# Attention work queued by products, values last, and a Strassen pair in both output projections of a two-layer decoder trunk

## The chip, the cores and the metric

The kernel runs on one core of one Trainium2 chip. The time is device microseconds of one execution; three runs of the kernel before are given by their median. TensorE (PE) multiplies, ScalarE (ACT) and VectorE (DVE) work on tiles in SBUF and PSUM, SyncE (SP) and GpSimd (POOL) issue the transfers here.

## The reference, cut to what matters

256 tokens of width 2048 pass through two layers, all in float32. What the kernel computes is, in order:

```python
hn = rms_norm(h, norm_mix[0])                       # layer 0
proj = hn @ w_in                                    # 2048 x 6144: RG-LRU and HGRN2 heads
mixed = concatenate([lru, hgrn], -1)                # each 1024 wide
h = h + mixed @ w_out                               # output projection, 2048 x 2048
h = h + square(relu(rms_norm(h) @ w1)) @ w2         # 2048 x 8192, 8192 x 2048
hn = rms_norm(h, norm_mix[1])                       # layer 1
q, k, v = split(hn @ w_qkv)                         # 16 heads of 128; partial rotary on q, k
s = q @ k.T * 128 ** -0.5 + log(multiplicity)       # three dilated windows merged into one mask
h = h + (softmax(s) @ v) @ w_o                      # output projection, 2048 x 2048
h = h + square(relu(rms_norm(h) @ w1b)) @ w2b
out = rms_norm(h, final_norm)
```

## The kernel before, in words

**Split operands.** TensorE multiplies in a rounded float32 form, so each operand is split into a high part and the rest. Weights come in units of 128 x 2048 float32 (1 MB): SP loads them into `raw` (three buffers), ScalarE casts the high part (`hi`, L103), VectorE subtracts it (`lo`, L104). Each block of 128 x 128 activations by 128 x 512 weights takes three matmuls (high by high, high by low, low by high), all issued by `mm` (L182). `fetch` prepares units two to three ahead, in the order of the list `units`.

**Two ways to multiply.** `tokens` takes one group of 512 output columns: four units, and for each unit and each half of the tokens (`j`) four blocks, twelve matmuls of 512 columns. These twelve are called a **product** here. Two groups cost 2 x 4 x 2 = 16 products. `blocks` takes a pair of column groups, `n0` and `n0 + 1`, and multiplies the first half of the inner dimension (blocks 0 to 7) by a seven-product scheme of Strassen's kind, the second half (units 8 to 15, called "n" in the lists) plainly: 7 + 8 = 15 products. The seven are called a, t1, t2, c, t3, d and t4. Their weights are sums of units: VectorE adds some (L131), an accumulating DMA of POOL's queue adds others (L143, L149). Their activations are sums too, the "forms" (`formx` for the first MLP matrix and the attention, `formh` for the second): four combinations of 128 x 128 blocks on VectorE (`combos`, L574 to L577) and a split (`part_forms`, L570 and L571). `ORDERS` lists the products: a, t1, then one n, t2, c, the other n, t3, d, n, t4, n. When a product of the seven is complete, an *event* reads its PSUM bank. In `first` (w1) `hold` copies it away on ScalarE (L697) into tiles `y1`, `y2`, `y4`; in `second` (w2) `to_x` adds it to the residual `xres` on VectorE (L732).

**The stages.** The recurrent layer runs to about 337 us. `out_project` then runs four groups of `tokens` against w_out. After each group the residual is added (L588), and `to_features` is put in the list `later`: it transposes the residual on TensorE (`turn`, L185) into a bank `pl` (two banks), scales by the gain and splits into `bufa` (L225 and L226), and for the first two groups also makes the forms by way of a tile `z` of the name `y21` (one buffer, L609). The MLP runs four quarters, each of two pairs by w1 and two by w2. Between them `to_h` transposes the squared activations into `bufb` and makes `formh`. At the end of layer 0 each finished group is turned into features for the attention (`done`).

**What sets the order.** `later` holds Python functions that issue instructions. `flush` runs all that were there when a plain unit began, after that unit: whole `to_features` calls, two halves at once, go between two products. Matmuls through `mm` and transposes through `turn` keep the order in which they are issued; each engine's other instructions are placed by a scheduler with priorities (`urgent` puts them early, `stream` puts the weights' work somewhat early).

**The attention.** Six pairs by w_qkv in the order `ATTENTION = "qvqqvq"`: a "q" pair gives queries and keys of four heads, a "v" pair the values of eight. `queries_keys` applies the rotary on VectorE (L876 to L880) and transposes on TensorE (L883), with a copy to `qT` and `kT` (L884). `scores` takes two matmuls (L891 and L892), adds the mask (L894), takes the maximum (L898), the exponential on ScalarE, and the division on VectorE (L902); it transposes the probabilities into the bank `pd` (L905) and copies them to `pT` (L907). `mix` multiplies by the values into the bank `po` (L913 and L914) and splits into `bufb` (L915). These transposes and matmuls are called on the engine directly, so the scheduler places them, without `urgent`. The residual waits in DRAM (`kept`) and POOL brings it back (L933). Then come `out_project` with w_o, the second MLP and the final norm.

Of the kernel before, what the change touches and what calls it, by code (L numbers as in the profile page):

```python
# [36 lines left out]
TC_ID, TC_LNC, TC_FREQ = 0, 128, 512  # L37
NTAB = 528
# [3 lines left out]
def trunk_kernel(ctx, tc, x, xtok, cols, tab, masks, pos, fin, w_in, w_gate, w_out, w_qkv, w_o, w1, w2, out):  # L42
# [28 lines left out]
    def plan2(src, i):  # L71
        for what, u in ORDERS[src is not w1]:
            units.append((src, None if u is None else i + u, what, i))
# [51 lines left out]
    def combine(u, src, i, what, i0):  # L125
# [115 lines left out]
    nc.sync.dma_start(tab_, tab)  # L241
    msk = cst.tile([P, NLEV, P], I8, name="msk")
    nc.sync.dma_start(msk, masks)
    ident = tab_[:, TC_ID:TC_ID + P]
    lnc = tab_[:, TC_LNC:TC_LNC + 384]
# [68 lines left out]
    def tokens(src, i0, mov, kgs=(0, 1, 2, 3), by_k=False):  # L314
        ks = range(KB)
        ps = [pmm.tile([P, 512], F32, name="p") for _ in range(2)]
        for g in kgs:
            w = unit(src, i0 + g)
            order = [(j, i) for i in range(4) for j in range(2)] if by_k else \
                [(j, i) for j in range(2) for i in range(4)]  # L320
            for j, i in order:
                k = ks[4 * g + i]
                h, l = w.part(i * 512, 512)
                xh = mov[:, k, j * P:j * P + P]
                xl = mov[:, k, S + j * P:S + j * P + P]
                first, last = g == kgs[0] and i == 0, g == kgs[-1] and i == 3
# [6 lines left out]
    def tokens_group(src, i0, rt=None, by_k=False, kgs=(0, 1, 2, 3)):  # L333
        ps = tokens(src, i0, bufa, kgs, by_k)
# [14 lines left out]
    wk = mixers.enter_context(tc.tile_pool(name="wk", bufs=2))  # L349
    nrm = FirstNorm()  # L350
# [3 lines left out]
    rs = tmp.tile([P, S], F32, name="nr", bufs=1)  # L354
# [238 lines left out]
    def to_features(n, gname, forms=None):  # L593
        def work():
            with urgent():
                for half in range(2):
# [6 lines left out]
                    if forms is None:  # L603
                        for i in range(2):
                            split_to(bufa[:, k + i], p[:, i], col(gname, k + i))
                        continue
                    z = pair.tile([P, 2, 2, P], F32, name="y21")
# [8 lines left out]
        later.append(work)  # L616

    def out_project(src, gname, kgs):
# [6 lines left out]
    nrm = out_project(w_out, "nmlp0", (2, 3, 0, 1))  # L625
    cosT = cst.tile([P, 2, 16], F32, name="cosT")
    sinT = cst.tile([P, 2, 16], F32, name="sinT")

    def blocks(src, i0, n0, mov, forms, events, final):
        plain = lambda j, k: (mov[:, k, j * P:j * P + P], mov[:, k, S + j * P:S + j * P + P])  # L630
# [20 lines left out]
        for what, u in ORDERS[src is not w1]:  # L651
# [8 lines left out]
            due = len(later)  # L660
# [4 lines left out]
            flush(due)  # L665

    def to_h(n, tiles):
# [20 lines left out]
        later.append(work)  # L688

    def first(i0, n0):  # L690
# [23 lines left out]
        def final(n, j, bank):  # L714
            with urgent():
                if (n, j) == (1, 1):
                    keep["delta"] = bank
                elif (n, j) == (0, 1):
                    y = pair.tile([P, 512], F32, name="y21")
# [6 lines left out]
        blocks(w1, i0, n0, bufa, formx, {"a": hold("y1", 2), "t1": hold("y4"), "t2": hold("y2"), "t3": u3}, final)  # L726

    def second(i0, n0, nrm, r2, r2n, done, gains):
        def to_x(bank, j, n, r, last):
            at = slice(n * 512, n * 512 + 512)  # L730
            with urgent():
                V.scalar_tensor_tensor(xres[:, j, at], bank, r[:, j:j + 1], xres[:, j, at], op0=OP.mult, op1=OP.add)  # L732
# [8 lines left out]
        def u3(bank):  # L741
# [3 lines left out]
        blocks(w2, i0, n0, bufb, formh,  # L745
               {"a": lambda b: to_x(b, 0, n0, r2, False), "t1": lambda b: to_x(b, 1, n0 + 1, r2, False),
                "t2": u2, "t3": u3},
               lambda n, j, b: to_x(b, j, n0 + n, r2, (n, j) != (1, 1)))
        done(n0)

    def mlp(layer, nrm, nxt, gname):
        fing = []

        def gains():
            for n, name in enumerate(("y1", "y1", "y2", "y4")):
                fing.append(pair.tile([P, 512], F32, name=name, bufs=2 if n < 2 else 1))
# [8 lines left out]
        for q in range(4):  # L765
# [17 lines left out]
            for n in (0, 2):  # L783
                second(layer * 64 + q * 16, n, ends, r2, r2n, done, gains if ends and not gname and not n else None)
        return fing

    def rotary():
# [19 lines left out]
        V.tensor_scalar(sinT, cosT, math.pi, -2.0 * math.pi, op0=OP.is_gt, op1=OP.mult)  # L807
        V.tensor_tensor(cosT, cosT, sinT, OP.add)
        V.tensor_scalar(cosT, cosT, PI, -PI, op0=OP.min, op1=OP.max)
        V.tensor_scalar(sinT, ang, PI, -PI, op0=OP.min, op1=OP.max)  # L810
        lut(cosT, cosT, AF.Sin)
        lut(sinT, sinT, AF.Sin)
# [8 lines left out]
    wk = mixers.enter_context(tc.tile_pool(name="wk2", bufs=2, reuse_waits="tile"))  # L821
    rt = rstd(nx1)
# [3 lines left out]
    def token_pair(i, c0, ready, raw=()):  # L826
        out_ = lambda n, j: xres[:, j, c0 + 512 * n:c0 + 512 * n + 512]
# [39 lines left out]
    def queries_keys(i, raw=()):  # L867
        turned = [wk.tile([P, 4, S], F32, name="qT", bufs=2), wk.tile([P, 4, S], F32, name="kT", bufs=2)]

        def ready(n, j, o):  # L870
# [3 lines left out]
            with urgent():  # L874
                b = wk.tile([P, 4, 2, 16], F32, name="rb", bufs=2)
                V.tensor_tensor(b[:, :, 0], r[:, :, 1], per(sinT), OP.mult)  # L876
                V.tensor_tensor(b[:, :, 1], r[:, :, 0], per(sinT), OP.mult)
                for two in range(2):
                    V.tensor_tensor(r[:, :, two], r[:, :, two], per(cosT), OP.mult)
                    V.tensor_tensor(r[:, :, two], r[:, :, two], b[:, :, two], OP.add if two else OP.subtract)  # L880
# [3 lines left out]
                A.copy(turned[n][:, :, j * P:j * P + P], p)  # L884
# [4 lines left out]
    def scores(q, k):  # L889
        ps_ = psc.tile([P, 384], F32, name="pl", bufs=2)  # L890
        T.matmul(ps_[:, :P], q[:, :P], k[:, :P], start=True, stop=True)  # L891
        T.matmul(ps_[:, P:], q[:, P:], k, start=True, stop=True)  # L892
        s = wk.tile([P, 384], F32, name="as", bufs=2)
        V.scalar_tensor_tensor(s, ps_, P ** -0.5, lnc, op0=OP.mult, op1=OP.add)  # L894
        nm = wk.tile([P, 2], F32, name="nm", bufs=2)
        ll = wk.tile([P, 2], F32, name="ll", bufs=2)
        for j, sl in enumerate((slice(0, P), slice(P, 384))):
            V.tensor_reduce(nm[:, j:j + 1], s[:, sl], AX.X, OP.max, negate=True)  # L898
            lut(s[:, sl], s[:, sl], AF.Exp, bias=nm[:, j:j + 1], accum_out=ll[:, j:j + 1])
        V.reciprocal(ll, ll)  # L900
        for j, sl in enumerate((slice(0, P), slice(P, 384))):
            V.tensor_scalar(s[:, sl], s[:, sl], ll[:, j:j + 1], None, op0=OP.mult)  # L902
        pt = psc.tile([P, 384], F32, name="pd", bufs=1)
        for j in range(3):
            T.transpose(pt[:, j * P:j * P + P], s[:, j * P:j * P + P], ident)  # L905
        st = wk.tile([P, 384], F32, name="pT", bufs=5)
        A.copy(st, pt)  # L907
        return st

    def mix(hd, st):  # L910
        vs = slice(D // 2 + (hd % 8) * P, D // 2 + (hd % 8) * P + P)
        po = psc.tile([P, S], F32, name="po", bufs=1)
        T.matmul(po, xres[:, 0, vs], st[:, :S], start=True, stop=False, skip_group_check=True)  # L913
        T.matmul(po[:, P:], xres[:, 1, vs], st[:, S:], start=False, stop=True, skip_group_check=True)  # L914
        split_to(bufb[:, hd], po)  # L915

    waiting, hd = [], 0
    for i, what in enumerate(ATTENTION):
        if what == "v":
            token_pair(i, D // 2, lambda *_: None)  # L920
        else:
            q, k = queries_keys(i, ((0, 0), (1, 1)) if not i else ())
            for h in range(4):
                waiting.append((hd, scores(q[:, h], k[:, h])))
                hd += 1
                if i and ATTENTION[:i].count("v") * 8 >= hd:
                    mix(*waiting.pop(0))
        if what == "v":
            while waiting:
                mix(*waiting.pop(0))  # L930
    for n in range(4):
# [5 lines left out]
    nrm = out_project(w_o, "nmlp1", (0, 1, 2, 3))  # L937
# [48 lines left out]
LINE = 64  # L986
# [4 lines left out]
ORDERS = (_A + (("n", 6),) + _B + (("n", 7),) + _C, _A + (("n", 7),) + _B + (("n", 6),) + _C)  # L991
T4_DMA = lambda w1, w2, w_qkv: (w1, w_qkv)
# [3 lines left out]
def _tables():  # L996
# [9 lines left out]
    tab = np.zeros((P, NTAB), np.float32)  # L1006
# [17 lines left out]
def _layout(a):  # L1024
# [32 lines left out]
    for what in ATTENTION:  # L1057
# [14 lines left out]
        "w_in": c(np.concatenate(w_in)), "w_gate": c(w_gate), "w_out": c(toks(n(a["rec_w_out"][0]))),  # L1072
        "w_qkv": c(np.concatenate(w_qkv)), "w_o": c(toks(n(a["attn_w_o"][0]))),
# [20 lines left out]
```

## Time and profile before

| what | value |
|---|---|
| runs of the kernel | 2190.3, 2188.92, 2190.04 us (median 2190.04) |
| profiled execution | 2187.37 us, span 2185.4 us |
| granted clock of TensorE, mean | 0.997 |
| TensorE / weight loads / VectorE / ScalarE / GpSimd busy | 2142.0 / 1814.9 / 1808.3 / 1301.5 / 60.1 us |
| HBM read / written | 475.44 / 4.19 MB |

The profile records one execution. A row of a timeline has start, duration, engine, line, operation, output and inputs with shapes; a bracket holds the idle time before it and what ended that. In the view of waits a row reads: who waited, for whom, total us, times, longest. Line numbers are those of the kernel before. "p", "pt", "po", "pd" and "pl" are PSUM banks. Matmuls overlap: one of 512 columns lasts 0.39 us in the records, while the next begins 0.23 us after its start.

### The profile page before, as it was taken

To read this page: it belongs to the slowest core of one execution; us is meant where nothing else is said; L and a number is where in the kernel's file an instruction comes from. 1 tells how busy PE (TensorE), PEld (TensorE's weight loads), DVE (VectorE), ACT (ScalarE), POOL (GpSimd) and SP (SyncE) were. 2 spreads that over 40 slices of the span, in tenths; PEclk is the share of its full clock that TensorE was granted. 3 is DMA by queue.
4 is the path that set the end of the run, shared out by engine and by line. 5 is a ranking of instruction groups with operands and counts; after the bars stand their busy time and mean duration, and the time that the engine had idled before them with its cause. 6 is when DMAs were issued, how large, how long until landed. Compare 5 with 4: busy or idle time off the path is not lost.

```text
span 2185.4 us, 27134 instructions
## 1 busy us (share of the span) xinstructions
PE 2142.0 (98%) x10778; PEld 1814.9 (83%) x10778; DVE 1808.3 (83%) x1972; ACT 1301.5 (60%) x1408; POOL 60.1 (3%) x77
## 2 busy tenths in 40 slices
PE   9999999999999999999989999999999999999997
PEld 8999998878888888888778888778888888888886
DVE  8766787779879889889888787767897898898897
ACT  7444485566566466566566565555655755755664
POOL 0000000000000000000000000000000000000000
PEclk9999999999999999999999999999999999999999
DMA  8444445577777777677766767747767777777873
GB/s 316 157 161 165 149 158 207 183 242 236 232 234 247 225 240 241 234 241 234 241 221 212 241 211 213 250 157 222 230 219 256 239 222 245 251 226 225 262 236 130
DMA packets 68734, 481.39 MB, mean 220 GB/s; under 512 B 7680, under 2 KB 8448, under 8 KB 11648
## 3 DMA queue, kind: packets, MB, share of 16 engines
q1 hardware_dynamic: 58176, 410.90, 51.6%
q0 software_dynamic: 10144, 68.16, 16.1%
q8 instruction: 84, 1.38, 0.3%
q10 hardware_dynamic: 288, 0.61, 0.1%
q14 instruction: 42, 0.34, 0.0%
HBM read 475.44 MB, written 4.19 MB: 219 GB/s over the span
## 4 chain that ended last, share of the span: by engine, by line
PE 86%; ACT 6%; DVE 4%; issue 2%; DMA 1%; SPq 0%; DVEq 0%; ACTq 0%
PE p L182 57%; PE po L182 11%; PE pd L182 10%; PE pt L182 4%; ACT hi L103 4%; DVE lo L104 2%; PE pl L185 2%; PE pl L453 1%; DMA raw<-in_w 0%; ACT y L701 0%; DMA raw<-in_w_qkv 0%; ACT formh L570 0%; ACT y L697 0%; ACT y L702 0%; PE pl L892 0%
## 5 line engine op out<-in xcount | busy, mean ns | idle before, releaser
L103 ACT CAST hi<-raw 128x2048 fp32r<-128x2048 f32 (+2 forms) x432 | 673.4, 1577 | 550.7 <-PE p L182 347.3
L104 DVE TENSOR_TENSOR lo<-raw,hi 128x2048 fp32r<-128x2048 f32 (+2 forms) x432 | 804.9, 1874 | 197.2 <-ACT hi L103 195.4
L182 PE MATMUL p<-hi,bufb 128*128 128x512 f32 x1408 | 450.1, 391 | 4.8 <-DVE xall L732 2.6
L182 PE MATMUL p<-hi,bufa 128*128 128x512 f32 x1360 | 439.6, 391 | 12.2 <-ACT y L697 7.9
L182 PEld LDWEIGHTS p<-hi,bufb 128*128 128x128 f32 x1408 | 264.2, 188 | 63.6 <-DVE xall L732 6.1
L182 PEld LDWEIGHTS p<-hi,bufa 128*128 128x128 f32 x1360 | 254.9, 188 | 69.7 <-ACT y L697 11.3
L104 DVE TENSOR_TENSOR lo<-s,hi 128x2048 fp32r<-128x2048 f32 x114 | 260.8, 2288 | 28.2 <-ACT hi L103 25.9
L182 PE MATMUL p<-lo,bufb 128*128 128x512 f32 x704 | 274.4, 390 | 1.2 <-DVE lo L104 1.2
L182 PE MATMUL p<-lo,bufa 128*128 128x512 f32 x680 | 266.5, 392 | 3.8 <-DVE lo L104 3.7
L103 ACT CAST hi<-s 128x2048 fp32r<-128x2048 f32 x114 | 218.1, 1913 | 57.4 <-PE po L182 24.0
L182 PE MATMUL p<-bufa,hi 128*128 128x256 f32 x1280 | 240.9, 287 | 0.1
L182 PEld LDWEIGHTS p<-bufa,hi 128*128 128x128 f32 x1280 | 200.7, 191 | 0.4 <-DVE hz L400 0.3
L182 PE MATMUL p<-bufa,lo 128*128 128x256 f32 x640 | 182.7, 285 | 0.0
L182 PEld LDWEIGHTS p<-lo,bufb 128*128 128x128 f32 x704 | 132.2, 188 | 28.5 <-DVE lo L104 1.6
L182 PEld LDWEIGHTS p<-lo,bufa 128*128 128x128 f32 x680 | 127.7, 188 | 32.7 <-DVE lo L104 6.9
L131 DVE TENSOR_TENSOR s<-s,raw 128x2048 f32<-128x2048 f32 x54 | 123.4, 2286 | 12.3 <-DMA raw<-in_w_qkv 9.8
L182 PEld LDWEIGHTS p<-bufa,lo 128*128 128x128 f32 x640 | 122.4, 191 | 0.0
L182 PE MATMUL p<-hi,formx 128*128 128x512 f32 x352 | 115.9, 390 | 0.0
L104 DVE TENSOR_TENSOR lo<-t,hi 128x2048 fp32r<-128x2048 f32 x38 | 87.0, 2289 | 17.7 <-ACT hi L103 17.7
L131 DVE TENSOR_TENSOR s<-raw,t 128x2048 f32<-128x2048 f32 x38 | 86.9, 2286 | 0.0
L182 PE MATMUL pd<-hi,bufa 128*128 128x512 f32 x256 | 84.8, 392 | 0.0
L182 PE MATMUL po<-hi,bufa 128*128 128x512 f32 x256 | 84.8, 392 | 0.0
(290 smaller groups left out, 3075.6 us busy)
## 6 DMA issues: line engine op xcount, KB each, us to landing
raw<-in_w SPq DMA_DIRECT2D x224, 1024.0 KB, 4.9
raw<-in_w_in SPq DMA_DIRECT2D x46, 1024.0 KB, 4.8
raw<-in_w_qkv SPq DMA_DIRECT2D x42, 1024.0 KB, 6.6
t<-in_w SPq DMA_DIRECT2D x32, 1024.0 KB, 5.4
t<-in_w POOLq DMA_DIRECT2D x32, 1024.0 KB, 8.6
raw<-in_w_out SPq DMA_DIRECT2D x16, 1024.0 KB, 4.7
s<-in_w POOLq DMA_DIRECT2D x16, 1024.0 KB, 8.7
raw<-in_w_o SPq DMA_DIRECT2D x16, 1024.0 KB, 4.8
```

The source lines that it names most:

```text
L103: A.copy(h, w)
L104: V.tensor_tensor(l, w, h.bitcast(F32), OP.subtract)
L131: V.tensor_tensor(held[to], held[x], held[y], OP.add)
L182: chain[:] = [after(T.matmul(*args, **kw), chain)]
L185: chain[:] = [after(T.transpose(out_, in_, ident), chain)]
L453: T.matmul(pl[:, j], kq[:, js], halves(qp[:, js], c, True), start=True, stop=True)
```

## The change

The change has these parts.

- `later` becomes a queue with due times. `clock` counts products, `put_off(wait, f)` makes `f` due `wait` products later, and `flush` after each product runs what is due, at most one function in `blocks` and two in `tokens`. `to_features` is put off by 2 products and each of its halves is a function of its own, `to_h` by 5.
- `out_project` runs two groups by `tokens` and the last two as one pair by `second` (with w_out or w_o, in the Strassen scheme). The forms of `bufb` are made in `formh` during the first group. The "t4" weights come by the accumulating DMA for all but w2.
- `y4` and `y21` get two buffers each; room is made by taking the mask table and some tiles out of the constant pool. All sources use one order of products.
- The attention's order is "qqvqqv". Transposes of queries and keys are put off by 5 products, the scores of head h of a pair by 6 + 2h, the transposes of the probabilities by 3 more, the mixes by 2 after the values, all through `mm` and `turn`. The softmax is marked urgent; its division moves to ScalarE. A mix's result is copied by ScalarE before the split, and mixes alternate between two banks. Rotary takes four operations for six. Every second query/key pair keeps one block in a spare tile.

The diff, cut to its core:

```diff
-    units.extend((w_out, 4 * n + g) for n in range(4) for g in (2, 3, 0, 1))
     for layer in range(2):
...
-            plan(w_o, 16)
+        plan((w_out, w_o)[layer], 8)
+        plan2((w_out, w_o)[layer], 8)
...
-        if ahead == ("t4",) and src not in T4_DMA(w1, w2, w_qkv):
+        if ahead == ("t4",) and src is w2:
             add("s", "s", "d")
...
-        if what == "c" and src in T4_DMA(w1, w2, w_qkv):
+        if what == "c" and src is not w2:
             nc.gpsimd.dma_start(held["s"], src[i0 + 1], accum_op=OP.add)
...
-    def flush(due=None):
-        todo = later[:due]
-        del later[:due]
-        for f in todo:
-            f()
+    clock = [0]
+
+    def put_off(wait, *fs):
+        later.extend((clock[0] + wait, f) for f in fs)
+
+    def flush(products, most):
+        clock[0] += products
+        later.sort(key=lambda x: x[0])
+        while most and later and later[0][0] <= clock[0]:
+            later.pop(0)[1]()
+            most -= 1
...
-            flush()
+                if i == 3 and (j or not by_k):
+                    flush(2 if by_k else 1, 2)
...
-                    z = pair.tile([P, 2, 2, P], F32, name="y21")
+                    z = pair.tile([P, 2, 2, P], F32, name="y21", bufs=2)
...
-        later.append(work)
+        put_off(WAIT_X, *(lambda half=half: work(half) for half in range(2)))
...
-        for n in range(4):
-            add_res(tokens(src, 4 * n, bufb, kgs), n, nrm)
-            to_features(n, gname, formx if n < 2 else None)
+        def forms(k):
+            z = pair.tile([P, 2, 2, P], F32, name="y21", bufs=2)
+            h, l = (bufb[:, k + off:k + off + 2, c * S:c * S + S].bitcast(F32) for c in range(2))
+            V.tensor_tensor(z.rearrange("p i j c -> p i (j c)"), h, l, OP.add)
+            a11, a21, a12, a22 = (z[:, i, j] for i in range(2) for j in range(2))
+            combos(a22, a11, a21, a12, a11, a21, a12, a22)
+            part_forms(formh, k // 2, 1, slice(0, 4), z.rearrange("p i j (one c) -> p one (i j) c", one=1))
+
+        put_off(4, *(lambda k=k: forms(k) for k in range(0, 8, 2)))
+        for n in range(2):
+            add_res(tokens(src, 4 * n, bufb, ks=[(k + off) % KB for k in PAIRED]), n, nrm)
+            to_features(n, gname, formx)
+        second(src, 0, 2, nrm, None, OP.subtract, lambda n: to_features(n, gname), None, off)
         return nrm
...
-            flush(due)
+                flush(1, 1)
...
-        later.append(work)
+        put_off(WAIT_H, work)
...
-        blocks(w1, i0, n0, bufa, formx, {"a": hold("y1", 2), "t1": hold("y4"), "t2": hold("y2"), "t3": u3}, final)
+        blocks(w1, i0, n0, bufa, formx, {"a": hold("y1", 2), "t1": hold("y4", 2), "t2": hold("y2"), "t3": u3}, final)
...
-                for h in range(4):
-                    T.transpose(p[:, h], t[:, h], ident)
-                A.copy(turned[n][:, :, j * P:j * P + P], p)
+                for h in range(4):
+                    turn(p[:, h], t[:, h])
+                with urgent():
+                    A.copy(turned[n][:, :, j * P:j * P + P], p)
+
+            put_off(WAIT_Q, turns)
...
-        for j, sl in enumerate((slice(0, P), slice(P, 384))):
-            V.tensor_scalar(s[:, sl], s[:, sl], ll[:, j:j + 1], None, op0=OP.mult)
...
+                for j, sl in enumerate((slice(0, P), slice(P, 384))):
+                    A.activation(s[:, sl], s[:, sl], AF.Copy, scale=ll[:, j:j + 1])
+            put_off(wait, lambda: turned(s))
...
-        po = psc.tile([P, S], F32, name="po", bufs=1)
-        T.matmul(po, xres[:, 0, vs], st[:, :S], start=True, stop=False, skip_group_check=True)
-        T.matmul(po[:, P:], xres[:, 1, vs], st[:, S:], start=False, stop=True, skip_group_check=True)
-        split_to(bufb[:, hd], po)
+        po = psc.tile([P, S], F32, name="pd" if hd % 2 else "po", bufs=1)
+        mm(po, xres[:, 0, vs], st[:, :S], start=True, stop=False, skip_group_check=True)
+        mm(po[:, P:], xres[:, 1, vs], st[:, S:], start=False, stop=True, skip_group_check=True)
+        z = tmp.tile([P, S], F32, name="z")
+        with urgent():
+            A.copy(z, po)
+        split_to(bufb[:, hd], z)
...
             token_pair(i, D // 2, lambda *_: None)
+            put_off(2, *(lambda h=h: mix(h, ready_.pop(h)) for h in range(hd - 8, hd)))
...
-                waiting.append((hd, scores(q[:, h], k[:, h])))
+                put_off(WAIT_Q + 1 + 2 * h, head(hd, q[:, h], k[:, h], WAIT_S))
...
+    restore(0)
+    restore(1)
+    put_off(2, lambda: restore(2), lambda: restore(3))
...
-ATTENTION = "qvqqvq"
+ATTENTION = "qqvqqv"
...
+WAIT_H, WAIT_X, WAIT_Q, WAIT_S = 5, 2, 5, 3
...
-ORDERS = (_A + (("n", 6),) + _B + (("n", 7),) + _C, _A + (("n", 7),) + _B + (("n", 6),) + _C)
+ORDERS = _A + (("n", 7),) + _B + (("n", 6),) + _C
```

More of the change, by code (lines that the diff above doesn't have):

```diff
@@ L325, in tokens @@
                 xl = mov[:, k, S + j * P:S + j * P + P]
-                first, last = g == kgs[0] and i == 0, g == kgs[-1] and i == 3
+                first, last = g == 0 and i == 0, g == 3 and i == 3
                 mm(ps[j], xh, h, start=first, stop=False)
@@ L593, in to_features, with work @@
     def to_features(n, gname, forms=None):
-        def work():
+        def work(half):
             with urgent():
-                for half in range(2):
+                if True:
                     p = psc.tile([P, 2, S], F32, name="pl", bufs=2)
@@ L718, in final @@
                 elif (n, j) == (0, 1):
-                    y = pair.tile([P, 512], F32, name="y21")
+                    y = pair.tile([P, 512], F32, name="y21", bufs=2)
                     relu2(0, 1, y, bank)
@@ L783, in mlp @@
             for n in (0, 2):
-                second(layer * 64 + q * 16, n, ends, r2, r2n, done, gains if ends and not gname and not n else None)
+                second(w2, layer * 64 + q * 16, n, ends, r2, r2n, done, gains if ends and not gname and not n else None)
         return fing
@@ L826, in token_pair, with out_ @@
     def token_pair(i, c0, ready, raw=()):
-        out_ = lambda n, j: xres[:, j, c0 + 512 * n:c0 + 512 * n + 512]
+        spare_ = wk.tile([P, 512], F32, name="q0", bufs=1) if not c0 and ATTENTION[:i].count("q") % 2 else None
+        def out_(n, j):
+            return xres[:, j, c0 + 512 * n:c0 + 512 * n + 512] if spare_ is None or (n, j) != (0, 0) else spare_
         def put(n, j, r=rt):
@@ L875, in ready @@
                 b = wk.tile([P, 4, 2, 16], F32, name="rb", bufs=2)
[L876 to L880, printed above, removed]
+                c = wk.tile([P, 4, 2, 16], F32, name="rc", bufs=2)
```

133 lines of the change are left out of this document (71 added, 62 removed).

## The prediction

> **What bounds the kernel now.** I read the page first: which engine is full, and which one the chain that ended last runs through.
>
> ```profile
> span 2185.4 us, 27134 instructions
> ...
> PE 2142.0 (98%) x10778; PEld 1814.9 (83%) x10778; DVE 1808.3 (83%) x1972; ACT 1301.5 (60%) x1408; POOL 60.1 (3%) x77
> ...
> PE 86%; ACT 6%; DVE 4%; issue 2%; DMA 1%; SPq 0%; DVEq 0%; ACTq 0%
> ```
>
> The reader is to see TensorE busy nearly throughout and on 86% of the chain. Two things can shorten this kernel: fewer matmuls, or fewer of TensorE's own waits. VectorE at 83% is second and matters below. The chain in order of time gives the price of matmuls:
>
> ```profile
> 559.25 5.44 PE p L182 x24
> ...
> 1106.52 4.38 PE po L182 x12
> ```
>
> Twenty-four 128x512 matmuls take 5.44 us, so one **product** of twelve takes 2.72 us. The second row is a product that took 4.38; I return to it. Next the view of TensorE's waits (total, times, longest), then the same view from 1145 to 1430 us, the attention, and last from 1065 to 1145, the passage into it:
>
> ```profile
> PE p L182 <- ACT y L697: 7.9, 8, 1.0
> PE pl L185 <- DVE bufa L226: 5.6, 1, 5.6
> ...
> PE p L182 <- DVE bufa L226: 3.6, 3, 1.4
> ```
>
> ```profile
> PE pl L891 <- ACT qT L884: 2.0, 1, 2.0
> PE p L182 <- ACT bufb L222: 1.9, 3, 1.4
> PE p L182 <- DVE lo L104: 1.4, 2, 1.1
> PE po L913 <- ACT pT L907: 0.9, 1, 0.9
> PE po L913 <- DVE bufb L223: 0.8, 1, 0.8
> ```
>
> ```profile
> PE p L182 <- DVE xall L732: 1.3, 1, 1.3
> PE p L182 <- DVE lo L104: 1.2, 1, 1.2
> ```
>
> The waits are few and named; nearly each has an edit of the change against it.
>
> **The change part by part.** The sum is made against the profiled execution: 2187.37 us, its span of 2185.4 and 2.0 around it. The median of the runs, 2190.04, lies 2.7 higher; I add that at the end.
>
> *Products (A).* A pair of column groups costs 16 products by `tokens` (2 groups x 4 weights x 2 halves) and 15 by `blocks`. Two projections save 2 x 2.72 = 5.4 us of TensorE. The price is on VectorE, whose durations come from the groups by line and shape:
>
> ```profile
> L104 DVE TENSOR_TENSOR lo<-raw,hi 128x2048 fp32r<-128x2048 f32 x266 | 609.1, 2290 | 143.5 <-ACT hi L103 142.3
> ...
> L131 DVE TENSOR_TENSOR s<-raw,t 128x2048 f32<-128x2048 f32 x38 | 86.9, 2286 | 0.0
> ...
> L226 DVE SCALAR_TENSOR_TENSOR bufa<-pl,c__83,bufa 128x256 fp32r<-128x256 f32 x24 | 10.6, 478 | 1.6 <-ACT bufa L225 1.3
> ...
> L223 DVE TENSOR_TENSOR bufa<-y,bufa 128x512 fp32r<-128x512 f32 x12 | 8.3, 691 | 0.0
> L571 DVE TENSOR_TENSOR formx<-y,formx 128x512 fp32r<-128x512 f32 x12 | 8.3, 688 | 2.9 <-ACT formx L570 2.9
> ...
> L577 DVE TENSOR_TENSOR y<-y 128x128 f32<-128x128 f32 x12 | 3.5, 291 | 0.3
> ```
>
> and its load from the view by stretches: a steady pair of the second MLP matrix, the last two pairs of layer 0's MLP, and a query/key pair.
>
> ```profile
> 514.64:556.37 41.73, 41.73 (x190) 34.62 (x188) 37.35 (x24) 23.89 (x17) 0.84 (x1) 1.00 0.70 226
> ...
> 1021.00:1062.56 41.56, 41.56 (x193) 34.55 (x192) 37.38 (x27) 25.60 (x23) 1.59 (x2) 1.00 0.73 239
> 1062.56:1116.21 53.65, 45.60 (x198) 36.92 (x196) 45.67 (x46) 30.95 (x36) 2.37 (x3) 0.94 0.64 215
> ...
> 1157.00:1208.00 51.00, 50.66 (x239) 41.81 (x239) 41.46 (x55) 33.62 (x41) 1.68 (x2) 1.00 0.73 235
> ```
>
> (columns: stretch and length, then busy time of PE, PEld, DVE, ACT, POOL, clock, DMA share, GB/s.) A steady pair holds VectorE 37.35 of 41.73 us and TensorE does not wait. The projection's new pair is that block less one add of 2.29 (the "t4" combination comes by an accumulating DMA), plus `to_features(1)` with its forms, 2 x (0.69 + 4 x 0.29 + 0.69) = 5.1, plus `to_features(3)`, 4 x 0.48 = 1.9: 42.0 us, in a block of 15 x 2.72 = 40.8 and some 2 of transposes. VectorE has no room left there. The forms of `bufb` (about 10 us: four times an add and a split of 0.69 each and four combinations of 0.29) come earlier, beside the `tokens` groups, whose weights need 2.29 per 5.44 us; I cost them at nothing under that cover, and up to 2 without it. The extra loads (18 of 1 MB for 16, two of them accumulating on POOL's queue) run at the steady pair's DMA share of 0.70 and are hidden likewise; behind them on POOL's queue stand only the last restores of the residual, needed several products later. What the full VectorE costs TensorE is not in the trace of before: between 0 and 4 us per pair, half of the 8.05 idle in 1062.56:1116.21, which VectorE filled to 45.67. I take 1 each, near the steady pair. A = 5.4 - 2.0 = **3.4**.
>
> *The second buffer of y4 (B).* Rows of ScalarE, VectorE and TensorE in the second pair of an MLP quarter:
>
> ```profile
> 645.52 1.91 ACT L103 CAST hi<-raw 128x2048 fp32r<-128x2048 f32 x1
> 647.33 0.61 ACT L570 CAST formh<-y 128x512 fp32r<-128x512 f32 x1
> 647.85 0.58 ACT L697 COPY y<-p 128x512 f32<-128x512 f32 x1
> ```
>
> ```profile
> 644.42 0.68 DVE L571 TENSOR_TENSOR formh<-y,formh 128x512 fp32r<-128x512 f32 x1
> ```
>
> ```profile
> 647.11 0.39 PE L182 MATMUL p<-hi,bufa 128*128 128x512 f32 x1
> 648.48 0.50 PE L182 MATMUL p<-hi,bufa 128*128 128x512 f32 x1 [0.99 <-ACT y L697]
> ```
>
> The bank of t1 was full at about 644.4, but its copy into y4 ran at 647.85: y4 still held the tile that L571 read until 645.1, and the copy had been queued behind two casts and a form. TensorE started 1.37 us after the matmul before, 0.23 being normal: 1.14 lost, eight times (the waits' 8), 9.1 us. With two buffers the copy can stand before those casts; even behind one running cast, 1.91 + 0.58 = 2.5 fits into the product of 2.72 that lies between. In the first pair of each quarter, where y4 is free, TensorE does not wait at that place. I take all: B = **9.1**. `to_h(1)` and `to_h(3)` come one product later; their readers are more than four products away.
>
> *Layer passage and features (C, D).* At 1099 the transposes of both halves of `to_features(3)` were issued at once, and the second four stood 5.6 us for a bank that VectorE (L226) emptied late. After it the stretch shows a clock of 0.94, and the quoted product took 4.38 for 2.72: 1.7 more. The change gives `y21` two buffers and issues one half per product, two products after the sums, so the bank is wanted seven products after its last user. VectorE's work stays: two pairs there need 37.38 + 45.67 = 83 us in some 85. So I leave the passage's 1.3 and 1.2 standing and charge 1.0: C = 5.6 + 1.7 - 1.0 = **6.3**. The three L226 waits of a product come from features asked for too soon (the two starts of an MLP and the first attention block); now `to_features(2)` goes out after products 2 and 3 of the next block and its readers are products 7 and 8. D = **3.6**.
>
> *Attention (E).* The five waits sum to 7.0. Transposes, scores and mixes now stand in TensorE's own fixed order, one per product; the mixes of eight heads go two per product into the output projection and no longer wait in a row. ScalarE gets the normalisation, which VectorE loses, and sixteen extra copies before the split. The nearest row is its cast of the same shape:
>
> ```profile
> L222 ACT CAST bufb<-po 128x256 fp32r<-128x256 f32 x16 | 5.9, 369 | 3.8 <-PE po L914 3.8
> ```
>
> At 0.37 each, 48 of these make 18 us over the attention, 4 to 5 per query/key pair, where 33.62 of 51 us are taken: hidden. New is a fixed wait: the transposes of the probabilities come three products (8.2 us) after the scores, and everything behind them on TensorE waits if the softmax is late. How long was the softmax? Heads 12 and 2 of before, score matmuls and VectorE's rows:
>
> ```profile
> 1409.23 0.60 PE L892 MATMUL pl<-kT,qT 128*128 128x256 f32 x2
> ```
>
> ```profile
> 1412.77 0.55 DVE L902 TENSOR_SCALAR as<-as,ll 128x128 f32<-128x128 f32 x2
> ```
>
> ```profile
> 1182.00 0.60 PE L892 MATMUL pl<-kT,qT 128*128 128x256 f32 x2
> ```
>
> ```profile
> 1187.74 0.55 DVE L894 SCALAR_TENSOR_TENSOR as<-pl,tab__181 128x384 f32<-128x384 f32 x1
> ...
> 1193.98 0.55 DVE L902 TENSOR_SCALAR as<-as,ll 128x128 f32<-128x128 f32 x2
> ```
>
> From the last score matmul to the last division 3.5 us in one, 11.9 in the other, of which 5.1 passed before VectorE began. The new code marks the softmax urgent, so I go by the shorter end, some 6 us with a cast and a subtraction in the way, and charge 2.0 for heads that come late; the ends are 0 and 16 x (11.9 - 8.2) = 59. E = 7.0 - 2.0 = **5.0**.
>
> The smaller table, `lnc` on POOL and the shorter rotary hide beside work or save below 1 us.
>
> Sum: 3.4 + 9.1 + 6.3 + 3.6 + 5.0 = 27.4. 2187.4 - 27.4 = 2160.0, and 2.7 more: **2162.7**, say 2163.
>
> The Trainium skill ("TensorE: Matmul & The Clock Gate", "What's actually happening") has the clock fall to half after an idle window of about 3.4 us; the trace agrees, with 0.94 around its one 5.6 us wait. By that rule 5.6 us would not be the whole price of such a wait, and new waits over 3.4 us would each cost a cold product as well: sixteen of them some 16 x 1.7 = 27 us, an estimate that is in no sum here.
>
> **The rivals.**
> 1. *VectorE's ceiling.* The new pairs and the passage are VectorE-bound, and each projection loses 4 us: A = 5.4 - 8.0 = -2.6, C falls by 3, E by 1. Gain 17.4: 2173. For it: 42.0 of 42.6. Against: the steady pair at 89% shows no wait.
> 2. *The copy stays late.* The hold is queued behind the casts for ScalarE's sake and B is lost: 2172. For it: the buffer was free at 645.1, the copy ran 2.7 later. Against: the order was fixed with the buffer still taken.
> 3. *All waits go,* those of 1.3 and 1.2 too, and nothing is charged: 27.4 + 2.0 + 1.0 + 2.5 + 2.0 = 34.9, so 2155.
> 4. *The softmax sets the pace* (the slower side). If its chain stays at head 2's 11.9 us, each of sixteen heads stops TensorE for 3.7: 59 us more, 59 - 29.4 = 30 slower, 2220. It turns the sign from a mean chain of 8.2 + 29.4 / 16 = 10.0 us. For it: the chain changes engine four times, each time perhaps behind a running cast (1.91) or subtraction (2.29). Against: VectorE spent 5.1 us of head 2's chain on work that was merely ahead in the order.
>
> The Trainium skill (same page, "Architectural detail") calls ScalarE's and VectorE's queues strictly first in, first out, and lets only weight loads pass matmuls on TensorE; by that a late softmax holds up all products behind it. The trace agrees: TensorE stood 2.0 us for L884 with products behind.
>
> **How the numbers follow.** Forecast 0.55, rival 1 0.19, rival 2 0.07, rival 3 0.11, rival 4 0.08. The range reaches from 2148, somewhat under rival 3, since the waits' own row gives 7.9 where the starts give 9.1, to 2179, past rivals 1 and 2; it leaves out rival 4 and tails. A measurement of this kernel tells about 0.2% (4.4 us) from no change. Faster by more than that: 0.90, all but rival 4 and a piece of rivals 1 and 2 together; within 0.2%: 0.03; slower: 0.07, rival 4 from 10 us on.
>
> **What would show it.** A: 192 matmuls less 12 per projection, and no L104 or L732 wait above 2 us in those pairs. B: the L697 row gone from TensorE's waits. C: no L185 wait near the passage and a clock of 1.00 there. D: the L226 row gone. E: no more than 2 us of TensorE's waits for the probabilities in all. I am wrong if TensorE's waits in the attention exceed 7 us, if VectorE's waits appear in the projections, or if the stage of layer 0's recurrence, which the change does not touch, differs by over 2 us.

## The result, and the profile after

The changed kernel takes **2152.7 us** (median of four runs, 2152.49 to 2153.95) against 2190.0 before: a ratio of 0.983, 95% interval 0.9815 to 0.9849, 37.3 us faster. The profiled execution took 2152.51 us. The page after, lines that answer to those shown of before:

```profile
span 2150.7 us, 27131 instructions
...
PE 2130.8 (99%) x10754; PEld 1809.5 (84%) x10754; DVE 1834.3 (85%) x1959; ACT 1333.4 (62%) x1454; POOL 64.1 (3%) x82
...
PE 93%; DVE 3%; DMA 2%; ACT 1%; issue 1%; SPq 0%; DVEq 0%; ACTq 0%
```

24 matmuls fewer; VectorE and ScalarE work 26 and 32 us more, and still the chain lies more on TensorE (93% for 86%). TensorE's waits after, in full:

```profile
PE p L182 <- DVE lo L104: 5.2, 5, 1.9
PE p L182 <- DVE xall L751: 2.2, 2, 1.3
PE po L241 <- DVE xp L509: 1.1, 1, 1.1
PE p L182 <- ACT gr L211: 0.7, 1, 0.7
PE p L182 <- DVE z L404: 0.3, 1, 0.3
```

The rows of before for ScalarE's `y` (7.9), the bank of the transposes (5.6), the features (3.6), `qT`, `pT` and `bufb` are all gone. The longest row left is that for `lo`. Where the time went is read from the view by stretches, cut at the first product of each stage. Before: projection by w_out, first MLP, attention, projection by w_o, second MLP with the end.

```profile
336.70:426.50 89.80, 89.80 (x411) 74.59 (x410) 61.27 (x81) 49.55 (x73) 0.87 (x1) 1.00 0.64 212
426.50:1116.20 689.70, 676.28 (x3041) 558.03 (x3040) 600.09 (x428) 423.34 (x360) 22.67 (x27) 1.00 0.73 234
1116.20:1394.90 278.70, 274.29 (x1278) 227.16 (x1276) 229.79 (x296) 171.03 (x189) 11.57 (x14) 1.00 0.72 228
1394.90:1497.70 102.80, 99.08 (x462) 81.25 (x461) 66.30 (x102) 55.07 (x91) 2.33 (x3) 1.00 0.56 187
1497.70:2185.40 687.70, 671.15 (x3017) 553.76 (x3015) 591.41 (x424) 415.09 (x348) 21.76 (x27) 0.99 0.72 228
```

After:

```profile
335.40:422.60 87.20, 87.20 (x399) 72.22 (x398) 79.05 (x106) 55.74 (x71) 2.58 (x3) 1.00 0.73 233
422.60:1098.30 675.70, 672.83 (x3042) 556.69 (x3041) 600.63 (x429) 424.59 (x360) 23.18 (x28) 1.00 0.74 239
1098.30:1375.80 277.50, 276.02 (x1296) 228.47 (x1295) 224.76 (x258) 192.19 (x249) 11.57 (x14) 1.00 0.73 234
1375.80:1468.80 93.00, 92.98 (x431) 77.18 (x430) 77.81 (x100) 57.34 (x78) 4.04 (x5) 1.00 0.68 217
1468.80:2150.70 681.90, 670.02 (x3017) 554.07 (x3015) 592.61 (x424) 415.90 (x348) 21.81 (x27) 1.00 0.72 231
```

Start 1.3, first projection 2.6, first MLP 14.0, attention and second projection together 11.0 (before, attention work reached into the projection, so these two are read as one), second MLP 5.8: 34.7 us of span. In VectorE's column the two projections cost 18 and 12 us more, and TensorE's stays as long as the stretch: nothing of that shows there.

### The profile page after: what moved, and what is told of

It is laid out like the page before. It is cut to its first block, busy times and chain, and to the rows that moved or that the text cites. A ratio compares the mean times of both kernels' runs of the same rounds, so it can differ in the third digit from the quotient of the medians.

```text
span 2150.7 us, 27131 instructions
## 1 busy us (share of the span) xinstructions
PE 2130.8 (99%) x10754; PEld 1809.5 (84%) x10754; DVE 1834.3 (85%) x1959; ACT 1333.4 (62%) x1454; POOL 64.1 (3%) x82
## 4 chain that ended last, share of the span: by engine, by line
PE 93%; DVE 3%; DMA 2%; ACT 1%; issue 1%; SPq 0%; DVEq 0%; ACTq 0%
PE p L182 60%; PE po L182 14%; PE pd L182 12%; PE pt L182 4%; PE pl L185 2%; DVE lo L104 2%; PE pl L457 1%; DMA raw<-in_w_in 1%; ACT hi L103 1%; PE pl L182 0%; DMA raw<-in_w 0%; DMA raw<-in_w_qkv 0%; DVE xall L751 0%; PE pd L185 0%; PE pd L441 0%
## 5 line engine op out<-in xcount | busy, mean ns | idle before, releaser
L182 PE MATMUL p<-hi,bufb 128*128 128x512 f32 x1264 | 407.3, 391 | 2.4 <-DVE xall L751 2.2
L104 DVE TENSOR_TENSOR lo<-s,hi 128x2048 fp32r<-128x2048 f32 x120 | 274.5, 2288 | 26.0 <-ACT hi L103 25.9
L182 PEld LDWEIGHTS p<-hi,bufb 128*128 128x128 f32 x1264 | 237.2, 188 | 54.7 <-DVE xall L751 5.6
L103 ACT CAST hi<-s 128x2048 fp32r<-128x2048 f32 x120 | 229.5, 1912 | 52.2 <-PE po L182 22.6
L182 PE MATMUL p<-lo,bufb 128*128 128x512 f32 x632 | 246.2, 390 | 1.9 <-DVE lo L104 1.9
L182 PEld LDWEIGHTS p<-lo,bufb 128*128 128x128 f32 x632 | 118.7, 188 | 26.3 <-DVE lo L104 2.2
L182 PE MATMUL po<-hi,bufb 128*128 128x512 f32 x320 | 103.7, 390 | 0.0
L182 PE MATMUL p<-hi,formh 128*128 128x512 f32 x288 | 94.5, 389 | 0.0
```

Source lines behind the costliest of these rows:

```text
L103: A.copy(h, w)
L104: V.tensor_tensor(l, w, h.bitcast(F32), OP.subtract)
L182: chain[:] = [after(T.matmul(*args, **kw), chain)]
```

## The experiments

Twelve kernels ran. All but one are the changed kernel with one edit; the times are medians, to be held against 2152.7. The runs of before that were timed beside them have medians of 2189.1 to 2190.6, and a stage that an edit does not touch still varies in the traces (the first MLP takes 675.5 to 676.3 in the changed kernel and in the four runs whose edit concerns the attention alone), so a difference of about 1 us is not read as one.

**Which part of the passage's gain is the buffer?** Two runs for step C, one with the halves together, one with `y21` single.

```diff
-        put_off(WAIT_X, *(lambda half=half: work(half) for half in range(2)))
+        put_off(WAIT_X, lambda: [work(half) for half in range(2)])
```

> The changed kernel with both halves of to_features in one function, so that eight transposes go at once, two products after the sums; y21 keeps two buffers. Theory (step C by spreading): the second half waits for a bank again, up to 5.6 us and a slow product, 2160. Rival (step C by the second buffer of y21): the banks are free in time, 2152.7 within 1.5.

Measured: **2152.9**, the same. With two buffers, spreading the halves bought nothing.

```diff
-                    z = pair.tile([P, 2, 2, P], F32, name="y21", bufs=2)
+                    z = pair.tile([P, 2, 2, P], F32, name="y21")
```

(the same in the other two places that allocate it)

> The changed kernel with one buffer of y21, halves still apart. Theory (step C by spreading): 2152.7 within 1.5. Rival (step C by the second buffer): the chain of sums through y21 is serial again, a wait of TensorE of several us near the passage into the attention, 2157 to 2162.

Measured: **2177.6**, 24.9 us slower, more than the rival had. TensorE's waits in this run, and the first of them in its timeline:

```profile
PE pl L185 <- ACT y L613: 11.7, 3, 6.0
PE pl L185 <- DVE bufa L231: 5.1, 1, 5.1
```

```profile
388.50 0.39 PE L182 MATMUL p<-hi,bufb 128*128 128x512 f32 x1
394.20 1.11 PE L185 MATMUL pl<-tab__181,xall 128*128 128x128 f32 x4 [5.30 <-ACT y L613]
```

The wait of before, with its price, is back, and a like one stands in each new Strassen pair (388 us is in the first projection): the copy out of the transposes' bank (L613) waits for the only `y21`, the bank stays full, and TensorE stops at the next transpose. So step C is the buffer alone, and without it step A would have cost time: the projections take 94.2 and 100.4 us in this run, where four groups each take 89.8 and 95.3 (`sixteen_b`, below).

**y4.**

```diff
-        blocks(w1, i0, n0, bufa, formx, {"a": hold("y1", 2), "t1": hold("y4", 2), "t2": hold("y2"), "t3": u3}, final)
+        blocks(w1, i0, n0, bufa, formx, {"a": hold("y1", 2), "t1": hold("y4"), "t2": hold("y2"), "t3": u3}, final)
```

(and one buffer where the last stage takes a tile of the same name)

> The changed kernel with one buffer of y4 again. Theory (step B: the buffer): the copy of t1's bank waits for VectorE's last read of the tile as before, eight waits of TensorE on ScalarE's y of about 1.0 us by the waits' row, 1.14 by the starts; 2152.7 + 9.1 = 2161.8. Rival (the new due times and the one order of products removed the wait, the buffer is idle): no such row, 2152.7 within 1.

Measured: **2167.1**, 14.4 slower. The wait's row, and the place in the timeline:

```profile
PE p L182 <- ACT y L713: 12.0, 8, 1.5
```

```profile
473.62 0.39 PE L182 MATMUL p<-hi,bufa 128*128 128x512 f32 x1
475.51 0.50 PE L182 MATMUL p<-hi,bufa 128*128 128x512 f32 x1 [1.50 <-ACT y L713]
```

Eight waits, as said, but 1.89 from start to start, so 1.66 lost each where before it was 1.14. In the changed kernel `to_h(1)` comes a product later and holds y4 longer; the buffer is worth more there than in the kernel before.

**The buffers alone, in the kernel before.** Its edit: two buffers each for `y4` and `y21`, and the tables moved as in the change to make room. No queue, no seven-product pair, the old attention.

> The kernel before with nothing changed but two buffers each for y4 and y21, and the room for them made as in the change (smaller table first, mask table and two tiles elsewhere). Theory (B and C are the buffers): TensorE's waits on ScalarE's y, 9.1 by the starts, and the 5.6 with the slow product behind it, 1.7, are gone: 2190.0 - 16.4 = 2173.6, 1.3 less if the gain at the start comes from the smaller table. Rival (C needs the queue with due times too): 2190.0 - 9.1 = 2181, the wait in the passage stays.

Measured: **2168.3**, 20.8 faster than the runs of before beside it (2189.1) and 4 to 5 us below the theory. Its stretches for the first MLP, the attention and the second MLP, and the rows of its waits that were not touched:

```profile
425.20:1099.50 674.30, 672.14 (x3041) 556.78 (x3040) 598.29 (x427) 423.07 (x360) 23.19 (x28) 1.00 0.76 238
1099.50:1380.70 281.20, 275.21 (x1277) 227.03 (x1276) 229.97 (x297) 171.11 (x189) 11.55 (x14) 1.00 0.73 230
...
1483.50:2165.70 682.20, 669.69 (x3017) 554.04 (x3015) 591.68 (x424) 415.02 (x348) 21.80 (x27) 1.00 0.73 230
```

```profile
PE p L182 <- DVE lo L104: 5.4, 7, 1.5
PE p L182 <- DVE bufa L226: 4.2, 3, 1.4
```

More than half of the whole gain is two tiles' second buffers: the first MLP falls from 689.7 to 674.3, the second from 687.7 to 682.2, as low as in the changed kernel, although the three waits for features (L226) still stand. The attention behind the passage takes 2.5 more than before (281.2 for 278.7), so not all that the first MLP gains is gained for good. The granted clock, 0.50 from 1104 to 1110 us before, is 1.00 throughout the passage here.

**Seven products for eight.** The first try kept one order of products and put both projections back to four groups.

> The changed kernel with both output projections as four groups of tokens, 16 products where the change takes 15, under the new queue. Theory (step A, as the trace after suggests, with no charge on VectorE): 24 matmuls more, 2152.7 + 5.4 = 2158.1. Rival (VectorE's ceiling: the new pairs give back what they save): below 2155, and then waits on lo in the projections of the changed kernel that go away here.

Measured: 2169.8. The edit was a poor one: with four groups the last features come last, yet unit 7 is multiplied first, and in this kernel its first product reads two blocks of features before they are written. TensorE also waited at both starts of the MLPs:

```profile
PE p L181 <- ACT bufa L229: 4.8, 2, 2.4
...
PE p L181 <- DVE bufa L230: 3.2, 2, 1.6
```

So it says nothing of step A; it shows why the change could use one order of products, since the pair finishes group 3 before group 2. The second try:

```diff
-        plan((w_out, w_o)[layer], 8)
-        plan2((w_out, w_o)[layer], 8)
+        plan((w_out, w_o)[layer], 16)
...
-        for n in range(2):
+        for n in range(4):
...
-        second(src, 0, 2, nrm, None, OP.subtract, lambda n: to_features(n, gname), None, off)
...
-ORDERS = _A + (("n", 7),) + _B + (("n", 6),) + _C
+ORDERS = (_A + (("n", 6),) + _B + (("n", 7),) + _C, _A + (("n", 7),) + _B + (("n", 6),) + _C)
```

> As the run sixteen, but the first MLP matrix takes its two plain units in the order of the kernel before (6, then 7), because the features of the last group come last when all four groups go through tokens. Theory (step A in full, no charge on VectorE): 24 matmuls, 2152.7 + 5.4 = 2158.1, and no waits at the starts of the MLPs. Rival (VectorE's ceiling gives the products back): below 2155.

Measured: **2156.7**, 4.0 slower, between the two expectations. Its stretches (projections and MLPs):

```profile
335.30:425.10 89.80, 89.80 (x410) 74.61 (x409) 59.63 (x82) 48.87 (x73) 0.87 (x1) 1.00 0.64 213
425.10:1099.90 674.80, 672.86 (x3042) 556.72 (x3040) 600.18 (x429) 424.43 (x360) 23.19 (x28) 1.00 0.75 238
...
1378.10:1473.40 95.30, 95.30 (x443) 79.45 (x441) 58.28 (x76) 50.44 (x80) 2.36 (x3) 1.00 0.61 199
1473.40:2154.40 681.00, 669.75 (x3017) 554.08 (x3015) 592.30 (x424) 415.63 (x348) 21.82 (x27) 0.99 0.73 230
```

In the changed kernel the projections are 2.6 and 2.3 shorter, 4.9 of the 5.4; but its MLPs are each 0.9 longer. That need not be the pairs' price: in this run w1's two plain units also stand in the other order. The stretches of the two new pairs in the changed kernel show VectorE below its ceiling:

```profile
379.85:422.58 42.73, 42.73 (x198) 35.35 (x196) 39.04 (x37) 28.48 (x31) 1.72 (x2) 1.00 0.73 226
1425.80:1468.80 43.00, 42.98 (x197) 35.38 (x196) 40.17 (x39) 28.87 (x31) 1.70 (x2) 1.00 0.72 224
```

**The softmax's three products.** Rival 4 was tried from three sides. First the setting of three products, put to one and to two:

```diff
-WAIT_H, WAIT_X, WAIT_Q, WAIT_S = 5, 2, 5, 3
+WAIT_H, WAIT_X, WAIT_Q, WAIT_S = 5, 2, 5, 1
```

> The changed kernel with the transposes of the probabilities one product after the scores where the change waits three. Theory (rival 4's mechanism is real, the three products cover it: the chains of the changed kernel measure 4.8 to 13.3 us, the shortest possible is 3.5): with 2.7 us each of sixteen heads waits at least 0.8 and up to some 4 us, 13 to 60 us more, 2166 to 2213. Rival (the scheduler shortens the softmax to fit): under 5 us more, below 2158.

Measured: **2209.1**, 56.4 slower and slower than before. Fourteen heads stood at one product (two, behind other work of the queue, at three). The wait for the probabilities, and the attention's stretch with the granted clock (third from the end):

```profile
PE pd L185 <- ACT as L937: 34.3, 14, 4.0
```

```profile
1099.40:1435.00 335.60, 298.65 (x1298) 240.10 (x1297) 227.19 (x257) 195.31 (x249) 11.58 (x14) 0.94 0.63 197
```

The attention grew by 58.1 us, of which the waits explain 34.3. The rest is mostly the clock: 0.06 of 335.6 us is some 20. One of the waits and what followed:

```profile
1164.86 0.39 PE L182 MATMUL p<-hi,bufa 128*128 128x512 f32 x1
1168.55 1.09 PE L185 MATMUL pd<-tab__181,as 128*128 128x128 f32 x3 [3.29 <-ACT as L937]
1169.29 0.78 PE L182 MATMUL p<-hi,bufa 128*128 128x512 f32 x1
1169.86 0.63 PE L182 MATMUL p<-lo,bufa 128*128 128x512 f32 x1
1170.29 1.05 PE L182 MATMUL p<-hi,bufa 128*128 128x512 f32 x2
1171.14 0.63 PE L182 MATMUL p<-lo,bufa 128*128 128x512 f32 x1
```

From 1169.86 on a matmul starts every 0.43 us instead of 0.23. Here the softmax took 4.5 to 7.0 us from the end of the last score matmul to that of the last division (mean 5.6), read from the timeline, where in the changed kernel it took 4.8 to 13.3 (mean 7.9). How much of the latter is slack that the scheduler used is not shown.

> The changed kernel with the transposes of the probabilities two products after the scores (5.4 us) where the change waits three and the run wait_s1 one. Theory (the softmax itself needs 4.5 to 7.0 us, mean 5.6, as in wait_s1; what lies above that in the changed kernel is slack): about half of the heads wait, 0.5 to 1 us each, no wait over 3.4 us, so no fall of the clock: 2152.7 + 3 to 8 = 2156 to 2161. Rival (the chains of 5.8 to 13.3 us of the changed kernel are needed): waits of 3 us and more for most heads and a falling clock, 2180 or above.

(the same edit with 2) Measured: **2157.8**, 5.1 slower, inside the theory's range.

```profile
PE pd L185 <- ACT as L937: 2.3, 3, 1.2
```

Three waits, none over 1.3. But the edit moved few heads. The scores of the next head fall due together with these transposes, `flush` lets out one function per product, and the scores were listed first. Counted in the traces, ten of the sixteen heads have three products between scores and transposes, four have four and only two have two; in the changed kernel twelve have three, two have four and two have five. The waits do not follow the distance either. One head of the two at two products waits, 1.25 us; the other does not; and the two waits of 0.5 are of heads with four products, as here:

```profile
1174.52 0.81 PE L182 MATMUL pl<-kT,qT 128*128 128x128 f32 x4
...
1188.28 0.84 PE L185 MATMUL pd<-tab__181,as 128*128 128x128 f32 x3 [0.50 <-ACT as L937]
```

So this run does not price two products for all heads, and that three is the least number is not shown. Its 5.1 us are not these waits alone: the first projection begins 1.3 later, and the clock fell once in layer 0 (last section).

Then the urgency:

```diff
-            with urgent():
+            if True:
                 V.scalar_tensor_tensor(s, ps_, P ** -0.5, lnc, op0=OP.mult, op1=OP.add)
```

> The changed kernel with the softmax not marked urgent. Theory of the prediction (the long chains of before came from the low priority): chains lengthen beyond three products and TensorE waits for the probabilities, 5 us or more in all, 2158 or above. Rival (the scheduler fits the softmax in anyway, since the transposes stand where they stand): no such wait, 2152.7 within 1.5.

Measured: **2157.2**, 4.5 slower. One head in sixteen came late, and the stretch around it shows the clock:

```profile
PE pd L185 <- ACT as L937: 2.3, 1, 2.3
```

```profile
1225.00:1240.00 15.00, 12.58 (x51) 9.78 (x51) 9.64 (x10) 7.64 (x14) 0.11 (x1) 0.89 0.71 210
```

A wait of 2.3 and 0.11 of 15 us, 1.7, behind it make 4.0. So the mark matters here for one head, not for all.

**Values last.** The old order of pairs under the new queue; what the last query/key pair leaves is issued in a row before the projection. In this kernel the mixes of heads 6 and 7 run after the second group's values began to overwrite the first's.

```diff
-ATTENTION = "qqvqqv"
+ATTENTION = "qvqqvq"
...
+    while later:
+        later.sort(key=lambda x: x[0])
+        later.pop(0)[1]()
```

> The changed kernel with the old order of pairs, qvqqvq, under the new queue; what the last query and key pair leaves (transposes, scores, mixes) is issued in a row before the projection. Theory (values last gives that work products to stand between): TensorE waits there for copies and softmax, 8 us or more, 2161 or above. Rival (the fixed places alone made the gain, the order of pairs none): 2155 or below.

Measured: 2183.0, 30.3 slower. The row of the stretch in which the rest is issued:

```profile
1376.00:1410.30 34.30, 17.25 (x56) 10.85 (x56) 10.40 (x26) 15.83 (x40) 0.70 (x1) 0.59 0.24 86
```

34 us without a product, at a clock of 0.59. The theory holds for this form of it; a queue that carries the last pair's work into the projection was not tried, because its tiles are released before.

**What is left at the passage.** The waits after, 2.15 and 1.06 us by the starts, lie in the last quarter of layer 0. Two tries to shorten them:

```diff
-        if ahead == ("t4",) and src is w2:
+        if False:
...
-        if what == "c" and src is not w2:
+        if what == "c":
```

> The changed kernel with the sum for t4 of the second MLP matrix by the accumulating DMA too, as for all other sources: 16 additions of 2.29 us leave VectorE, 16 MB more come by POOL's queue. Theory (what is left of TensorE's waits at the passage and at the end, 2.15 + 1.06 + 1.5 by the starts, is VectorE's full queue): two thirds of it go, 2152.7 - 3 = 2149.7. Rival (the transfers are the limit, VectorE stood 2.1 us for one there): the extra transfers come late and TensorE waits more, 2155 or above.

Measured: **2153.0**, the same, although VectorE was relieved of 35 us:

```profile
PE 2131.2 (99%) x10754; PEld 1810.2 (84%) x10754; DVE 1798.8 (84%) x1943; ACT 1333.2 (62%) x1454; POOL 77.7 (4%) x98
```

```profile
PE p L182 <- DVE lo L104: 5.3, 7, 1.6
PE p L182 <- DVE xall L751: 2.2, 2, 1.3
```

Neither expectation: the waits stay nearly as they were. And the forms as a function of their own, put off by three more products:

> The changed kernel with the sums and forms of to_features as a function of their own, put off by three products more. Theory (VectorE is full at the passage as a whole, the place of the forms moves nothing): 2152.7 within 1.5. Rival (the forms stand in the way of lo and of the banks' readers at a bad moment): the waits of 2.15 and 1.06 shrink, 2150 or below.

Measured: 2153.2, the same, as the theory had it.

## Why the prediction was right, point by point

The time lay inside the range and 10 us under the forecast of 2163. Of these, 2.5 are the step from one execution to the median: I added 2.7, but the profiled execution after stands at its own median (2152.51 and 2152.71). The rest are the terms. In number, rival 3 (2155, given 0.11) came nearer than the forecast; its picture did not hold, since `lo` and `to_x` still wait at the passage and D did not come. Of the charges of 2.0, 1.0 and 2.0 only A's was paid, and that in part.

- **A, 3.4: measured 4.0** (`sixteen_b`; 4.8 when both kernels are held against the runs of before beside them). VectorE, with 39 to 40 us of work in 43 per pair, 2 to 3 less than the 42.0 that I summed (for a block of 42.8 by the same sum; rival 1 writes 42.6), did not hold up the projections. The charge of 2.0 was too large where the pairs stand, 0.5 there; the 1.8 in the MLPs may come from the order of the plain units. Rival 1 did not come about.
- **B, 9.1: right.** The row is gone, and `buffers` takes 5.4 from the second MLP, four waits of 1.14 and a little. In the changed kernel the buffer is worth 14.4, because the change itself puts the last read of y4 a product later: a term can be larger in the new kernel than in the old.
- **C, 6.3: mis-sized and for half the reason.** I named two causes, the second buffer and the spread over products. `halves` shows the spread worth nothing, `y21_one` and `buffers` show the buffer doing it all. In `buffers` the first MLP gains 15.4, so after B's share some 10, and some 8 when the attention's 2.5 is taken off. At the passage, the waits of 1.3 and 1.2 that I left standing as VectorE's ceiling mostly went as well in that run (0.7 on `lo` is left).
- **D, 3.6: the row went, the time did not come.** `buffers`, with those waits, has both MLPs together at 1356.5, the changed kernel at 1357.6. At the passage the changed kernel loses 2.15 and 1.06 on `lo` and `to_x`, where `buffers` loses 0.9; that this is where the features' time went is argued, as no run takes D out by itself. The third of the three waits, 0.9 before, lies in the attention's stretch and so in E.
- **E, 5.0: measured about 8** (attention and second projection, 381.5 to 373.5 in `sixteen_b`). The waits' row said 7.0, and with D's 0.9 it is 7.9. I charged 2.0 for late heads; not one was late, and that was partly luck. I took some 6 us for the softmax and 8.2 for the cover. The chains measure 7.9 in the mean and five of sixteen exceed 8.2; but the transposes came 8.4 to 15.5 us after the scores, since the queue held some back further, the two chains of 13.3 among them. Rival 4's mechanism is real: with fourteen heads at one product it costs 56 us.
- **The start** gave 1.3 that I did not forecast. The first projection begins between 335.3 and 336.7 in the runs of this study, the smaller table in all but the first, `wait_s2` with the smaller table at 336.7 again, so this is mostly how executions differ.

Left open: why VectorE runs late at the passage. It is not the sum for t4, not the place of the forms. In the changed kernel VectorE stands 2.1 us there for a transfer, and SP, which issues it, stands for VectorE to free a buffer of weights; a fourth buffer, which would tell, was not tried.

## What to carry to other kernels

When the chain lies on the matmul engine, read who its waits name, then ask which tile keeps that engine from answering: two second buffers alone gave 21 of 37 us here, and in the changed kernel they are worth 14.4 and 24.9, each taken out by itself. Work queued by count needs a distance that covers its latency with the others' queues in the way. Count the distance that comes out, in the trace: here the setting of two left fourteen of sixteen heads three or four products away, and the setting of one cost more than the whole change gains. A wait on the matmul engine can cost more than itself, by the slow clock behind it.

## What the runs showed of the hardware that was not expected

The clock fell after waits shorter than the one that the trace of before had shown (5.6 us): in `calm` after a single one of 2.3, in `wait_s1` to a mean of 0.94 over 336 us with no wait over 4.0. By the rule quoted in the prediction from the Trainium skill ("TensorE: Matmul & The Clock Gate", "What's actually happening"), the half clock comes after an idle window of about 3.4 us. These runs show that less idle can do. The length of a wait does not decide it alone, and short transposes need not stand behind it. The four us after a wait for `lo` at the passage, 2.13 us long in `wait_s2` and 1.90 in the changed kernel, with matmuls of 512 columns behind it in both:

```profile
1061.87:1065.87 4.00, 4.00 (x11) 3.20 (x12) 4.00 (x5) 2.58 (x4) 0.00 (x0) 0.59 0.72 263
```

```profile
1060.27:1064.27 4.00, 3.23 (x15) 2.48 (x15) 4.00 (x5) 3.08 (x6) 0.00 (x0) 1.00 0.76 265
```

After the wait at the same place the clock was 0.58 in `early_v` (1.92 us) and 0.61 in `wait_s1` (1.83 us), and it stayed at 1.00 after one of 2.03 us in the attention of before, which short score matmuls follow. What decides is open.

The estimate made in the prediction for sixteen late heads, 27 us for the clock, compares with some 20 in `wait_s1`; there ten of the fourteen waits, those of 2.3 us and more, were followed by a slow clock, and the four of 1.4 were not.
